# Even tokens first, and a two-phase convolution whose ScalarE/GpSimd taps are all of one sum

## The chip, the core and the metric

The kernel runs on one core of one Trainium2 chip. The metric is the device time of one execution in microseconds (us); lower is better. The core has five engines that run their own instruction queues in order and meet through semaphores: TensorE (PE, with its weight loads shown as PEld), VectorE (DVE), ScalarE (ACT), GpSimd (POOL) and SyncE (SP, which here issues all DMAs). Matrix products land in PSUM, everything else stands in SBUF or in DRAM scratch.

## What is computed

A trunk of two residual layers over 2048 tokens of width 1024, fp32, then a final RMSNorm. Layer 0 is gated linear attention (GLA), layer 1 a causal Conformer convolution module; each has a SiLU gate branch z.

```python
def conv_mixer(h, w_in, dw_w, dw_b, ln_w, ln_b, w_out):
    a, gl, z = jnp.split(h @ w_in, 3, axis=-1)
    u = a * jax.nn.sigmoid(gl)
    u = lax.conv_general_dilated(          # depthwise, causal, 31 taps
        u, dw_w.reshape(CONV_K, 1, CONV_E).astype(u.dtype),
        window_strides=(1,), padding=[(CONV_K - 1, 0)],
        dimension_numbers=('NWC', 'WIO', 'NWC'),
        feature_group_count=CONV_E) + dw_b
    u = jax.nn.silu(layernorm(u, ln_w, ln_b))
    return (u * jax.nn.silu(z)) @ w_out

for i in range(DEPTH):                     # 0: gla_mixer, 1: conv_mixer
    h = rmsnorm(x, norm_w[i])
    y = gla_mixer(h, ...) if i % N_MIXERS == 0 else conv_mixer(h, ...)
    x = x + y
return rmsnorm(x, final_norm_w)
```

The depthwise convolution is done for even and odd tokens apart. With `ue`, `uo` the even and odd tokens of u, A = even taps (16) on `ue`, B = odd taps (15) on `uo`, and C = (even + odd taps, 16) on `ue + uo`: the even outputs are A + B delayed by one, the odd outputs are C - A - B. That is 47 taps over 512 columns in place of 62.

## The kernel before

Activations stand transposed, 128 channels on the partitions and tokens along the free axis, in blocks of 512 tokens (`NB`); the 2048 tokens are two halves (`hf` 0 and 1) of two blocks each (`b`). Every product is done as three fp32r matmuls (hi x hi, hi x lo, lo x hi; `mm3`, line 144), 24 of 128x512 for one 128-channel output block. Weights come in units of 256 columns: a DMA into `wr`, a cast on ACT to `wh` (line 124) and the remainder `wl` on POOL (line 125), two buffers each.

**Layer 0** takes the first 868 us of the trace. In `core`, `turn` transposes each 128-token output `g` on PE into a PSUM bank (line 413), ACT copies it to `st` (line 418) and SP writes it to the scratch `gd` (line 422); head 3 stays in SBUF. `out1` reads it back, projects it, adds x (loaded by line 520) and stores x1 to scratch.

**Layer 1** has, per half, eight `u` units (one channel block of 128 each: `glu`, two projections and a product on DVE, line 754) and four `z` units (`gate_z`, SiLU on ACT, stored to scratch), in the order of `SCHED`. Once a channel block's u is complete (three buffers of u), `conv` puts its convolution on a background list `bg`, in pieces that `pump` hands out against a credit of PE time; LayerNorm goes to a list `bg2` (half 0, run beside half 1's convolution) or `held` (half 1, run beside the output projection). The pieces set only the order in which code is written; a scheduler with its own estimate of times then sets the order of instructions on each engine, with `high_priority` for the projections.

**A channel's convolution** (lines 598 to 677). The first `SIDES[hf][c]` taps of A, and as many of B, are "side" taps: ACT makes the products (line 622), POOL adds them up in `convA`, `convB` (line 624). The rest run on DVE as a chain of scalar_tensor_tensor (line 638) that accumulates in a PSUM bank (`b_bank`, two banks in all), started from the side sum in SBUF (line 642) and ended by writing the sum back to `convA` or `convB`. A comes first, then `ue += uo` (line 669, on POOL in half 0, on DVE in half 1), then B, then the even outputs on POOL (line 647), then C, started by subtracting from `convA` (line 640), and the odd outputs on DVE (line 652). POOL then sums the outputs into `S1` for LayerNorm (line 659).

**The end.** `out2` projects y for half 0, then half 1, adds x1 (`load_x`, line 825, into the buffers u, prod and d), sums squares (lines 842, 844), and `finish` scales by the final RMSNorm (line 864) and stores the block (line 865). LayerNorm of half 1 (lines 700 to 729) and the splitting of its y (line 190) run beside `out2(0, ...)`, on the same DVE, ACT and POOL queues.

## Time and profile before

| | |
|---|---|
| median of 3 runs | 1676.16 us (1675.92 to 1680.72) |
| the profiled execution's own time | 1678.1 us |
| its span in the profile | 1676.0 us |
| PE busy | 1609.4 us (96%) |
| DVE busy | 972.7 us (58%) |
| POOL busy | 900.2 us (54%) |
| ACT busy | 739.6 us (44%) |
| chain that ended last | PE 73%, DVE 16%, DMA 3%, ACT 3% |

Busy shares are means over stages with different limits, so the stretches of layer 1 are read apart further down. A matmul's shown duration overlaps the next one's; the pitch from start to start is what it costs. The same holds for DVE, by less. PEclk is the clock that TensorE was granted, as a share of 2.4 GHz: of its two levels, 1.2 and 2.4 GHz, a mean of 0.96 in a stretch is a mixture.

### The profile page before, as it was taken

Reading aid. Unit: us, or ns where it says so; the run is one execution under the profiler, and the core shown is the slowest. Engines: PE = TensorE matmul, PEld = TensorE weight load, DVE = VectorE, ACT = ScalarE, POOL = GpSimd, SP = SyncE. Lnnn points to the kernel's source line nnn. Section 1 sums busy time; section 2 is a strip of 40 time slices with the busy share of each in tenths; the row PEclk is TensorE's granted clock in tenths of the full one; section 3 lists DMA queues with packets and bytes.
Section 4 is the critical chain, followed back from the end, with each engine's and each line's share of the span. In section 5 each row is a group of like instructions: output and inputs, shape, how many; then the busy total and the mean of one; then the engine's idle time right before and its main releaser. Section 6 shows DMA issues by size and latency. Waiting matters only on the chain.

```text
span 1676.0 us, 23547 instructions
## 1 busy us (share of the span) xinstructions
PE 1609.4 (96%) x9028; PEld 1410.2 (84%) x9028; DVE 972.7 (58%) x1481; ACT 739.6 (44%) x1246; POOL 900.2 (54%) x787
## 2 busy tenths in 40 slices
PE   8999999999999999999999999999999899999697
PEld 6989999998889999999888887877788678877597
DVE  7433232241434232325243999989699999977634
ACT  6645252342557353415232544443553355435432
POOL 4444343334744333323342989985398798456342
PEclk9999999999999999999999999999999999999798
DMA  6021111144511212123452211225154113643633
GB/s 190 26 83 57 64 51 57 57 139 139 169 45 33 82 51 64 45 63 102 144 164 88 76 38 38 94 70 157 59 174 157 57 45 101 202 163 124 234 115 137
DMA packets 74016, 165.68 MB, mean 99 GB/s; under 512 B 7760, under 2 KB 16464, under 8 KB 73904
## 3 DMA queue, kind: packets, MB, share of 16 engines
q1 hardware_dynamic: 73904, 164.19, 30.5%
q8 instruction: 70, 1.15, 0.3%
q14 instruction: 42, 0.34, 0.1%
HBM read 128.51 MB, written 35.65 MB: 98 GB/s over the span
## 4 chain that ended last, share of the span: by engine, by line
PE 73%; DVE 16%; DMA 3%; ACT 3%; issue 2%; POOL 2%; SPq 0%; POOLq 0%; DVEq 0%; ACTq 0%
PE mm L144 63%; DVE pb L638 10%; PE pb L144 3%; PE pb L388 1%; PE pb L390 1%; DVE pb L642 1%; PE pm L379 1%; DMA wr<-in_wall_dram 1%; PE pm L413 1%; DVE u L754 1%; DVE al L190 1%; PE pm L288 1%; POOL acc L205 1%; DMA u<-x_scratch 1%; DVE pb L640 1%
## 5 line engine op out<-in xcount | busy, mean ns | idle before, releaser
L144 PE MATMUL mm<-ah,wh 128*128 128x512 f32 (+1 forms) x1600 | 595.3, 388 | 44.8 <-DVE u L838 20.4
L144 PE MATMUL mm<-al,wh 128*128 128x512 f32 (+1 forms) x1600 | 592.6, 385 | 0.0
L144 PE MATMUL mm<-ah,wl 128*128 128x512 f32 (+1 forms) x1600 | 590.0, 386 | 0.0
L125 POOL TENSOR_TENSOR wl<-wr,wh 128x1024 fp32r<-128x1024 f32 x140 | 344.0, 2471 | 214.9 <-ACT wh L124 208.9
L144 PEld LDWEIGHTS mm<-ah,wh 128*128 128x128 f32 x1600 | 302.3, 190 | 110.1 <-DVE u L838 20.0
L144 PEld LDWEIGHTS mm<-al,wh 128*128 128x128 f32 x1600 | 302.2, 190 | 57.1 <-issue 0.2
L144 PEld LDWEIGHTS mm<-ah,wl 128*128 128x128 f32 x1600 | 301.4, 190 | 58.0 <-issue 0.2
L144 PE MATMUL mm<-wh,ah 128*128 128x256 f32 x896 | 259.2, 289 | 0.0
L144 PE MATMUL mm<-wh,al 128*128 128x256 f32 x896 | 254.7, 284 | 0.0
L144 PE MATMUL mm<-wl,ah 128*128 128x256 f32 x896 | 254.2, 284 | 0.0
L124 ACT ACTIVATE wh<-wr 128x1024 fp32r<-128x1024 f32 x144 | 145.5, 1051 | 140.9 <-PE mm L144 92.4
L638 DVE SCALAR_TENSOR_TENSOR pb<-u,C,pb 128x512 f32<-128x512 f32 x252 | 184.9, 747 | 0.7
L638 DVE SCALAR_TENSOR_TENSOR pb<-u,dwc,pb 128x512 f32<-128x512 f32 x240 | 179.9, 750 | 1.2
L144 PEld LDWEIGHTS mm<-wl,ah 128*128 128x128 f32 x896 | 171.4, 191 | 0.4
L144 PEld LDWEIGHTS mm<-wh,ah 128*128 128x128 f32 x896 | 171.3, 191 | 0.4
L144 PEld LDWEIGHTS mm<-wh,al 128*128 128x128 f32 x896 | 171.3, 191 | 0.0
L622 ACT ACTIVATE prod<-u,C 128x512 f32<-128x512 f32 x148 | 105.5, 721 | 135.7 <-POOL convA L624 68.4
L624 POOL TENSOR_TENSOR convA<-convA,prod 128x512 f32<-128x512 f32 x74 | 98.3, 1329 | 5.7 <-ACT prod L622 1.6
L624 POOL TENSOR_TENSOR convB<-convB,prod 128x512 f32<-128x512 f32 x74 | 98.0, 1325 | 4.0 <-ACT convB L620 0.7
L397 DVE SCALAR_TENSOR_TENSOR S<-S,dec,pb 128x256 f32<-128x256 f32 x56 | 26.8, 479 | 95.4 <-PE pb L144 95.3
L401 POOL TENSOR_TENSOR ss<-ss,e 128x1 f32<-128x1 f32 x64 | 13.4, 209 | 124.4 <-ACT g L400 124.4
L523 DVE TENSOR_TENSOR Q<-mm,Q 128x512 f32<-128x512 f32 x32 | 22.1, 689 | 93.0 <-PE mm L144 78.3
(195 smaller groups left out, 2174.1 us busy)
## 6 DMA issues: line engine op xcount, KB each, us to landing
wr<-in_wall_dram SPq DMA_DIRECT2D x144, 512.0 KB, 4.1
raw<-in_xT_dram SPq DMA_DIRECT2D x32, 256.0 KB, 3.7
Q<-in_xT_dram SPq DMA_DIRECT2D x32, 256.0 KB, 3.2
x_scratch<-Q SPq DMA_DIRECT2D x32, 256.0 KB, 3.1
sz_scratch<-t SPq DMA_DIRECT2D x32, 256.0 KB, 2.3
b<-sz_scratch SPq DMA_DIRECT2D x32, 256.0 KB, 3.5
g_scratch<-st SPq DMA_DIRECT2D x48, 128.0 KB, 1.9
raw<-g_scratch SPq DMA_DIRECT2D x24, 256.0 KB, 3.5
```

Source lines behind the costliest of these rows:

```text
L124: act.activation(wh[:, ks, :], raw, AF.Copy)
L125: (dve if i < 2 else pool).tensor_tensor(wl[:, ks, :], raw, wh[:, ks, :].bitcast(F32), ALU.subtract)
L144: pe.matmul(ps, s, m, start=(i == 0), stop=(i == 3 * n - 1))
L190: dve.tensor_tensor(lo, src, hi.bitcast(F32), ALU.subtract)
L205: eng.tensor_tensor(acc, acc, sq, ALU.add)
L288: pe.matmul(ps, wgs[:, k, :], m, start=(n == 0), stop=(n == 15))
L379: pe.matmul(s_ps[:, 0:192], ki[:, js], Q[:, j].rearrange("p s c -> p (s c)"), start=True, stop=True)
L397: dve.scalar_tensor_tensor(S[h], S[h], dec[:, j:j + 1], kv, ALU.mult, ALU.add)
L523: dve.tensor_tensor(xr, ps, xr, ALU.add)
L622: act.activation(p, src, AF.Copy, scale=w)
L624: pool.tensor_tensor(acc, acc, p, ALU.add)
L638: dve.scalar_tensor_tensor(dstm, src, w, ps, ALU.mult, ALU.add)
```

## The change

Three things are changed together.

1. **Token order.** From layer 0's output on, each block of 512 tokens stands with its 256 even tokens first and its 256 odd ones behind. `turn` makes this order: the PE transpose writes token columns alternately to the two halves of a 256-column field of the PSUM bank. The stores to `gd` go in runs of 128 columns in place of 256, the residual of `out1` is read from `xP`, a second copy of x in the new order that the host makes, and the host puts the result back in order. In layer 1 the product of `glu` then reads and writes contiguous halves, and so does the product with z; before, `glu` wrote even and odd tokens alternately to two rows of u.
2. **Side taps.** All side taps are of A (`SIDES` doubled, but 18 becomes 15 once in each half), and B has none.
3. **Order and place.** B runs first on DVE, started by a tensor_scalar with the bias; then A, whose sum stays in its PSUM bank; then, with no store to `convA`, the even outputs on DVE from that bank (line 648 of the changed kernel), `ue += uo` always on POOL (line 670), and C goes on in the same bank (lines 643 and 637).

```diff
-SIDES = ((1, 7, 7, 7, 7, 5, 9, 7),
-         (1, 5, 3, 5, 9, 7, 6, 4))
+SIDES = ((2, 14, 14, 14, 14, 10, 15, 14),
+         (2, 10, 6, 10, 15, 14, 12, 8))
...
-                o = c * 256 + (i % 2) * P
-                pe.transpose(gt[:, o:o + P], g[:, c * P:(c + 1) * P], ident)
+                o = (i % 2) * CK
+                gv = gt[:, c * 256:(c + 1) * 256].rearrange("p (s t) -> p s t", s=2)[:, :, o:o + CK]
+                pe.transpose(gv.rearrange("p s t -> p t s"), g[:, c * P:(c + 1) * P], ident)
...
-                            out=gd[hf, r0:r0 + P, (i - 1) * P:(i + 1) * P],
-                            in_=st[:, c * 256:(c + 1) * 256])
+                            out=gd[hf, r0:r0 + P, b * NB:(b + 1) * NB].rearrange(
+                                "p (s t) -> p s t", s=2)[:, :, o:o + P],
+                            in_=st[:, c * 256:(c + 1) * 256].rearrange("p (s t) -> p s t", s=2))
...
-                    sp.dma_start(out=xr, in_=xT[ch * P:(ch + 1) * P, t0:t0 + NB])
+                    sp.dma_start(out=xr, in_=xP[ch * P:(ch + 1) * P, t0:t0 + NB])
...
-        def side(which):
-
-            st[which] = l2p.tile([P, NB + 1], F32, name="conv" + which, bufs=2)
-            acc = st["p" + which] = st[which][:, 1:NB + 1]
+        def side():
+
+            acc = st["pA"] = l2p.tile([P, NB], F32, name="convA", bufs=2)
             for m in range(nside):
-                src, w = tap(which, m)
+                src, w = tap("A", m)
                 p = acc if m == 0 else l2p.tile([P, NB], F32, name="prod", bufs=2)
-                if m == 0 and which == "B":
-                    act.activation(p, src, AF.Identity, scale=w, bias=cc(C_DWB, c))
-                else:
-                    act.activation(p, src, AF.Copy, scale=w)
+                act.activation(p, src, AF.Copy, scale=w)
...
-                first = 0 if which == "C" else nside
-                if m0 == first:
-                    st["ps"] = b_bank()
-                ps = st["ps"]
+                first = nside if which == "A" else 0
+                if m0 == first and which != "C":
+                    st["ps" + which] = b_bank()
+                ps = st["ps" + ("B" if which == "B" else "A")]
...
-                    if m == n - 1 and which != "C":
-                        dstm = st["p" + which]
+                    dstm = st["B"][:, 1:NB + 1] if which == "B" and m == n - 1 else ps
...
-                    elif which == "C":
-                        dve.scalar_tensor_tensor(dstm, src, w, st["pA"], ALU.mult, ALU.subtract)
+                    elif which == "A":
+                        dve.scalar_tensor_tensor(dstm, src, w, st["pA"], ALU.mult, ALU.add)
+                    elif which == "B":
+                        dve.tensor_scalar(dstm, src, w, cc(C_DWB, c), ALU.mult, ALU.add)
                     else:
-                        dve.scalar_tensor_tensor(dstm, src, w, st["p" + which], ALU.mult, ALU.add)
+                        dve.scalar_tensor_tensor(dstm, src, w, ps, ALU.mult, ALU.subtract)
...
-            pool.tensor_tensor(d[:, 0], st["pA"], st["B"][:, 0:NB], ALU.add)
+            dve.tensor_tensor(d[:, 0], st["psA"], st["B"][:, 0:NB], ALU.add)
...
-        for which, n in (("A", 16), ("B", 15), ("C", 16)):
-            m0 = 0 if which == "C" else nside
+        for which, n in (("B", 15), ("A", 16), ("C", 16)):
+            m0 = nside if which == "A" else 0
...
-                items.append((0.0, lambda: (pool if hf == 0 else dve).tensor_tensor(ue, ue, uo, ALU.add)))
-            if which == "B":
-                items.append((0.0, even))
+                items.append((0.0, lambda: pool.tensor_tensor(ue, ue, uo, ALU.add)))
+                items.append((0.6, even))
...
-                zv = z.rearrange("p (t s) -> p s t", s=2)
+                zv = wide(z)
...
-                    u[:, :, o:o + 256].rearrange("p s t -> p t s"),
-                    a_ps.rearrange("p (t s) -> p t s", s=2),
-                    sg.rearrange("p (t s) -> p t s", s=2), ALU.mult)
+                    u[:, :, o:o + 256],
+                    a_ps.rearrange("p (s t) -> p s t", s=2),
+                    sg.rearrange("p (s t) -> p s t", s=2), ALU.mult)
```

The order of instructions in layer 0 is the same before and after; only shapes differ there. In layer 1 it moves, and three places matter. In the rows a line number is the kernel's own, so the same statement can have another number before and after (638 and 637, 652 and 653, 669 and 670, 190 and 192, 167 and 169).

DVE in half 0, where one channel's last sum C ends and the next one's begins; before: line 652 is the odd output of a channel, 754 the product of `glu`, 640 the first tap of C, 642 the first tap of A behind the side sum.

```order
L652 SCALAR_TENSOR_TENSOR d<-pb,dwb_96,convB 128x512
L754 TENSOR_TENSOR u<-mm,t_9744 128x256x2
L754 TENSOR_TENSOR u<-mm,t_9820 128x256x2
L638 SCALAR_TENSOR_TENSOR pb<-u,C,pb 128x512
L640 SCALAR_TENSOR_TENSOR pb<-u,dwc,convA 128x512
L638 SCALAR_TENSOR_TENSOR convB<-u,C,pb 128x512
L638 SCALAR_TENSOR_TENSOR pb<-u,dwc,pb 128x512
L642 SCALAR_TENSOR_TENSOR pb<-u,C,convA 128x512
L638 SCALAR_TENSOR_TENSOR pb<-u,dwc,pb 128x512
L638 SCALAR_TENSOR_TENSOR pb<-u,C,pb 128x512
```

The same place of the changed kernel: line 639 is the first tap of A, 648 the even output, 653 the odd output, 641 the first tap of B, 643 the first tap of C.

```order
L639 SCALAR_TENSOR_TENSOR pb<-u,C,convA 128x512
L637 SCALAR_TENSOR_TENSOR pb<-u,dwc,pb 128x512
L637 SCALAR_TENSOR_TENSOR pb<-u,C,pb 128x512
L637 SCALAR_TENSOR_TENSOR pb<-u,dwc,pb 128x512
L648 TENSOR_TENSOR d<-pb,convB 128x512
L637 SCALAR_TENSOR_TENSOR pb<-u,dwc,pb 128x512 x4
L653 SCALAR_TENSOR_TENSOR d<-pb,dwb_96,convB 128x512
L754 TENSOR_TENSOR u<-mm,t_9949 128x2x256
L754 TENSOR_TENSOR u<-mm,t_10024 128x2x256
L641 TENSOR_SCALAR pb<-u,C 128x512
L643 SCALAR_TENSOR_TENSOR pb<-u,dwc,pb 128x512
```

What moved: before, C of a channel began behind B of the same channel, one row into the alternation with the next channel's A; now A, the even output, the rest of the channel before, two products of `glu` and the first tap of the next B stand between A's last tap and C's first, which needs `ue += uo` from POOL.

POOL in half 0, around `ue += uo`; before: line 669 is that addition, 624 the side sums, 647 the even output, 649 a carried column, 125 the weight remainder.

```order
L796 COPY halo<-u 128x30
L669 TENSOR_TENSOR u<-u 128x527
L624 TENSOR_TENSOR convA<-convA,prod 128x512
L647 TENSOR_TENSOR d<-convA,convB 128x512
L649 COPY bcar<-convB 128x1
L624 TENSOR_TENSOR convA<-convA,prod 128x512 x2
L624 TENSOR_TENSOR convB<-convB,prod 128x512 x4
L125 TENSOR_TENSOR wl<-wr,wh 128x1024 x2
```

The same place of the changed kernel: 670 is the addition, 625 the side sums, 650 the carried column, 785 the copy of the halo into a new u, 660 the sum for LayerNorm.

```order
L625 TENSOR_TENSOR convA<-convA,prod 128x512
L650 COPY bcar<-convB 128x1
L625 TENSOR_TENSOR convA<-convA,prod 128x512
L785 COPY u<-halo 128x2x15
L625 TENSOR_TENSOR convA<-convA,prod 128x512
L670 TENSOR_TENSOR u<-u 128x527
L660 TENSOR_TENSOR S_9658<-S_9658,d 128x1024
L676 COPY convB<-bcar 128x1
```

What moved: the even output has left POOL's queue, and the addition stands behind a halo copy and a side tap, where before it had the whole of B's chain between it and the first tap that needs it.

DVE near the end, where `out2` of half 0 finishes its first block (line 167 makes its variance just ahead of the first row here) and LayerNorm of half 1 goes on; before: 727 scales by LayerNorm's factor, 729 multiplies by z, 190 splits y, 844 sums squares, 864 scales and so frees the output block.

```order
L727 TENSOR_TENSOR d<-d,pm 128x2x256 x8
L729 TENSOR_TENSOR b_13753<-b_13753,d 128x2x256
L729 TENSOR_TENSOR b_13812<-b_13812,d 128x2x256
L190 TENSOR_TENSOR al<-b_13753,ah 128x512
L190 TENSOR_TENSOR al<-b_13803,ah 128x512
L190 TENSOR_TENSOR al<-b_13812,ah 128x512
L190 TENSOR_TENSOR al<-b_13821,ah 128x512
L844 TENSOR_TENSOR acc<-acc,pb 128x512 x2
L729 TENSOR_TENSOR b_13830<-b_13830,d 128x2x256
L844 TENSOR_TENSOR acc<-acc,pb 128x512
L729 TENSOR_TENSOR b_13848<-b_13848,d 128x2x256
L864 SCALAR_TENSOR_TENSOR u<-u,C,pb 128x512 x2
```

The same place of the changed kernel: 169 makes the variance, 192 is the split of y, 709 a sum of LayerNorm, 838 adds x1 to a projection.

```order
L169 TENSOR_SCALAR v_14041<-pb 128x4
L192 TENSOR_TENSOR al<-b_13653,ah 128x512
L192 TENSOR_TENSOR al<-b_13666,ah 128x512
L709 TENSOR_TENSOR S_12023<-S_12023,pb 128x2x256
L729 TENSOR_TENSOR b_13721<-b_13721,d 128x512
L192 TENSOR_TENSOR al<-b_13708,ah 128x512
L192 TENSOR_TENSOR al<-b_13721,ah 128x512
L844 TENSOR_TENSOR acc<-acc,pb 128x512 x2
L838 TENSOR_TENSOR d<-mm,d 128x512 x2
L192 TENSOR_TENSOR al<-b_13734,ah 128x512
L864 SCALAR_TENSOR_TENSOR u<-u,C,pb 128x512 x6
```

What moved: the block's scaling (864) came behind LayerNorm's second block (727 x8 and what follows it), and now stands ahead of all of that.

## Rows read from the trace of the kernel before

**Rows 1.** The whole span, by stretch of the program: layer 0 with its projection (0 to 868), half 0 of the convolution (925 to 1225), half 1 (1225 to 1475) and the end with LayerNorm beside the output projection (1475 to 1600). Columns: length, then busy us (and instructions) of each engine, mean granted TensorE clock, DMA share, GB/s. The last row is one slice of 25 us of the same view in which PE was never late.

```profile
0.00:868.00 868.00, 854.94 (x5535) 783.62 (x5535) 310.11 (x562) 385.03 (x737) 353.24 (x407) 1.00 0.28 86
...
925.00:1225.00 300.00, 288.68 (x1248) 236.14 (x1247) 277.22 (x369) 142.76 (x204) 239.81 (x179) 0.98 0.25 80
1225.00:1475.00 250.00, 240.49 (x1052) 197.04 (x1051) 249.97 (x340) 115.94 (x160) 192.15 (x135) 0.99 0.39 127
1475.00:1600.00 125.00, 103.27 (x451) 84.02 (x450) 80.37 (x117) 56.45 (x82) 64.20 (x35) 0.90 0.46 154
...
1050.00:1075.00 25.00, 25.00 (x112) 20.71 (x111) 24.61 (x35) 11.09 (x16) 24.26 (x19) 1.00 0.31 104
```

**Rows 2.** The same view of parts of the convolution: the units of half 0 up to 1100.

```profile
925.00:1100.00 175.00, 172.38 (x759) 141.87 (x758) 172.34 (x234) 86.49 (x122) 164.44 (x127) 1.00 0.20 66
```

**Rows 3.** PE's waits, engine, line and tile waited for, us in total, times, longest; the first row from 925 to 1225, the next from 1225 to 1475, the last from 1475 to 1600.

```profile
PE mm L144 <- DVE u L754: 5.8, 3, 3.2
...
PE mm L144 <- DVE u L754: 6.8, 3, 4.4
...
PE mm L144 <- DVE u L838: 18.2, 3, 16.2
```

**Rows 4.** DVE from 925 to 1475, grouped by line: operation, out<-in, shapes, count, then busy us, mean ns of one, and idle time before them with what ended it.

```profile
L638 DVE SCALAR_TENSOR_TENSOR pb<-u,C,pb 128x512 f32<-128x512 f32 x252 | 184.9, 747 | 0.7
...
L642 DVE SCALAR_TENSOR_TENSOR pb<-u,C,convB 128x512 f32<-128x512 f32 x16 | 26.5, 1654 | 5.2 <-POOL convB L624 5.2
L640 DVE SCALAR_TENSOR_TENSOR pb<-u,dwc,convA 128x512 f32<-128x512 f32 x16 | 26.0, 1626 | 0.0
L642 DVE SCALAR_TENSOR_TENSOR pb<-u,C,convA 128x512 f32<-128x512 f32 x16 | 21.3, 1331 | 0.9 <-ACT convA L622 0.9
...
L669 DVE TENSOR_TENSOR u<-u 128x527 f32<-128x527 f32 x8 | 11.2, 1399 | 0.0
```

**Rows 5.** The same view over the whole span, shapes kept apart: the product of `glu`, a contiguous product of a PSUM and an SBUF operand (line 523), a tensor_scalar of 512 columns with two per-partition scalars (line 313), a sum of an SBUF and a PSUM operand (line 709), and the PE transposes of `turn`.

```profile
L754 DVE TENSOR_TENSOR u<-mm,t 128x512 f32<-128x512 f32 x32 | 33.2, 1071 | 22.8 <-PE mm L144 22.8
L523 DVE TENSOR_TENSOR Q<-mm,Q 128x512 f32<-128x512 f32 x32 | 22.1, 689 | 93.0 <-PE mm L144 78.3 <-DMA Q<-in_xT_dram 14.7
L313 DVE TENSOR_SCALAR Ei<-pm,C 128x512 f32<-128x512 f32 x14 | 9.9, 746 | 2.7 <-ACT tmp L312 2.4
L709 DVE TENSOR_TENSOR S<-S,pb 128x512 f32<-128x512 f32 x16 | 10.8, 685 | 6.8 <-ACT pb L706 4.0 <-POOL S L709 2.7
L413 PE MATMUL pm<-ident,g 128*128 128x128 f32 x128 | 24.4, 272 | 0.0
```

**Rows 6.** The timeline of DVE at the end of half 1's convolution (start, length, engine, line, operation, count): taps of two chains in turn, and then seven of one chain.

```profile
1469.12 0.74 DVE L638 SCALAR_TENSOR_TENSOR pb<-u,C,pb 128x512 f32<-128x512 f32 x1
1469.78 0.74 DVE L638 SCALAR_TENSOR_TENSOR pb<-u,dwc,pb 128x512 f32<-128x512 f32 x1
...
1473.73 5.49 DVE L638 SCALAR_TENSOR_TENSOR pb<-u,dwc,pb 128x512 f32<-128x512 f32 x7
```

**Rows 7.** POOL from 925 to 1475, grouped by line as in rows 4.

```profile
L125 POOL TENSOR_TENSOR wl<-wr,wh 128x1024 fp32r<-128x1024 f32 x50 | 124.4, 2500 | 50.6 <-ACT wh L124 50.6
L624 POOL TENSOR_TENSOR convA<-convA,prod 128x512 f32<-128x512 f32 x74 | 98.3, 1329 | 5.7 <-ACT prod L622 1.6 <-ACT convA L622 0.7
L647 POOL TENSOR_TENSOR d<-convA,convB 128x512 f32<-128x512 f32 x16 | 22.3, 1397 | 27.0 <-DVE convB L638 25.9 <-ACT prod L622 1.2
...
L669 POOL TENSOR_TENSOR u<-u 128x527 f32<-128x527 f32 x8 | 11.1, 1391 | 0.3 <-DVE convA L638 0.3
```

**Rows 8.** POOL's waits ahead of its halo copies from 925 to 1475, columns as in rows 3.

```profile
POOL u L785 <- DVE pb L638: 19.6, 5, 13.9
```

**Rows 9.** PE's timeline in layer 0, around one pair of transposes.

```profile
201.38 0.38 PE L413 MATMUL pm<-ident,g 128*128 128x128 f32 x2
201.51 0.48 PE L144 MATMUL mm<-ah,wl 128*128 128x512 f32 x1
201.82 0.40 PE L144 MATMUL mm<-ah,wh 128*128 128x512 f32 x1
```

**Rows 10.** DVE's timeline near the end, from the first block's variance to the first sum with x1 of the last half.

```profile
1547.89 0.15 DVE L167 TENSOR_SCALAR v<-pb 128x4 f32<-128x4 f32 x1
1548.70 4.87 DVE L727 TENSOR_TENSOR d<-d,pm 128x512 f32<-128x512 f32 x8 [0.66 <-PE pm L178]
...
1570.08 1.39 DVE L864 SCALAR_TENSOR_TENSOR u<-u,C,pb 128x512 f32<-128x512 f32 x2
...
1581.36 1.29 DVE L838 TENSOR_TENSOR u<-mm,u 128x512 f32<-128x512 f32 x2 [1.49 <-DMA u<-x_scratch]
```

**Rows 11.** The chain of waits over the same stretch (start, length, what).

```profile
1570.08 1.41 DVE u L864 x2
...
1571.50 3.56 DMA out_dram<-u
...
1575.08 6.19 DMA u<-x_scratch
...
1581.36 0.70 DVE u L838
```

22 lines of the change are left out of this document (13 added, 9 removed).

## The prediction

> **What bounds the kernel now.** I read the mean busy shares first: PE is at 96% of the span, so no edit of another engine can give back more than PE's late moments and its slow ones. Then the stretches [rows 1]. In layer 0 PE is busy for 854.94 of 868 us while DVE is below half: PE sets the pace, and the change moves no instruction there. In the convolution both are full: from 925 to 1225 PE is busy 288.68 of 300 us and DVE 277.22, and from 1225 to 1475 DVE is busy 249.97 of 250 us. DVE sets the pace there, through the product of `glu` that PE waits for [rows 3]. From 1475 to 1600 PE loses most: it is busy 103.27 of 125 us, and one wait of 16.2 us for `out2`'s sum with x1 is most of it [rows 3].
>
> How much is there to win? A slice where PE was never late holds 112 matmuls in 25 us, 0.2232 us each [rows 1]. At that pitch 925 to 1225 has room for 1344 instructions and holds 1248: 96 x 0.2232 = 21 us lost, of which 11.3 us are idle and the rest is mainly matmuls at the lower clock (granted 0.98). In the same way 1225 to 1475 lost 68 x 0.2232 = 15 us (9.5 us idle) and 1475 to 1600 lost 109 x 0.2232 = 24 us (21.7 us idle, granted 0.90). A few records can be missing and some of those counted are narrower, so the idle times are the lower ends. Together 43 to 60 us are the ceiling.
>
> **DVE, part by part.** In the convolution a tap is shown with 0.747 us [rows 4], but taps of two chains in turn start 0.66 us apart, and seven of one chain take 5.49 us, 0.78 each [rows 6]: a tap that reads what the one ahead wrote pays 0.12 us more.
> - First tap of B: 1.654 us with the side sum in SBUF [rows 4] becomes a tensor_scalar. The nearest row, of the same width with two scalars but from PSUM, is 0.746 us [rows 5]. From SBUF the trace shows none; the ends are 0.4 us (half of that row and a little) and 1.331 us, the cheapest first tap with only SBUF inputs [rows 4]. I take 0.746: 8 x 0.908 = 7.3 us per half.
> - First tap of A keeps its form. First tap of C reads PSUM in place of `convA`: 1.626 us becomes 0.747 [rows 4], 8 x 0.879 = 7.0 us per half.
> - `glu`: 1.071 us with alternating writes, 0.689 for a contiguous product of the same operands [rows 5]: 16 x 0.382 = 6.1 us per half.
> - Added: eight even outputs per half (0.685 us shown [rows 5], about 0.6 in the queue), 4.8 us; side taps fall from 100 to 97 in half 0 and from 80 to 77 in half 1, three more DVE taps each, 2.0 us. By the written order 69 taps stand directly behind the one they read, 57 before: 6 x 0.12 = 0.7 us per half.
> - In half 1 `ue += uo` leaves DVE: 8 x 1.399 = 11.2 us [rows 4].
>
> Half 0: 7.3 + 7.0 + 6.1 - 4.8 - 2.0 - 0.7 = 12.9 us less. Half 1: 12.9 + 11.2 = 24.1 us less.
>
> **POOL and ACT.** A chain's first side product needs no addition, so one chain in place of two saves one in each channel less: 84 additions in half 0 become 97 - 8 = 89, 64 in half 1 become 69. Five more cost 5 x 1.33 = 6.6 us per half; the even outputs leave, 8 x 1.397 = 11.2 us; `ue += uo` comes in half 1, 8 x 1.391 = 11.1 us [rows 7]. Half 0 is 4.6 us lighter, half 1 6.5 us heavier. That weight is covered in half 1, where POOL is busy 192.15 of 250 us [rows 1], and would be paid in full if it came to stand ahead of C. ACT makes six products fewer and has slack: nothing.
>
> **What of it reaches the end.** In half 0 up to 1100, POOL is busy 164.44 of 175 us, nearly as full as DVE with 172.34 [rows 2]. A pace that DVE alone would allow, 12.9 us faster, is held back by POOL, so I take 8 us. In half 1 DVE gives more than PE has to lose; I take 10 us, near the idle 9.5, since some slow-clock time stays.
>
> The new order adds a wait: C's first tap (643) needs `ue += uo` (670), which POOL can do only behind A's last tap. On DVE a tap, the even output, four taps, the odd output, two products and B's first tap stand between: 0.66 + 0.6 + 4 x 0.78 + 0.66 + 1.2 + 0.66, some 7 us. On POOL stand two side additions, a halo copy and the addition itself, 4 us. But the halo copy waits for the u buffer that the channel before frees with its last C tap (such waits cost 19.6 us before [rows 8]); from there POOL needs 1.33 + 1.39 = 2.7 us and DVE has 2.6 us of other work. So it is nearly even, and I charge 0.25 us a channel, 16 x 0.25 = 4 us. The ends are nothing, and two weight remainders of 2.5 us each [rows 7] ahead of it. What queues behind that tap on DVE is the next `glu`, and so PE.
>
> The end: before, the scaling that frees `out2`'s buffers starts 22.2 us behind its variance (1547.89 to 1570.08) because LayerNorm's second block stands ahead of it [rows 10]; store, load and sum then take until 1581.36 [rows 11], and PE has waited 16.2 us [rows 3]. Now eleven instructions of 0.6 to 0.9 us stand between, about 8 us, 14 us less, and LayerNorm's second block comes behind. Of the 16.2 us I take 13; the ends are nothing, if LayerNorm's waits on ACT and on z's load now stand ahead of the last half's sums, and the whole 24 us.
>
> **Layer 0.** 128 transposes write PSUM alternately 1 KB apart. A pair and one matmul take 201.82 - 201.38 = 0.44 us, of which the matmul is 0.23: 0.105 us for one [rows 9], 13.4 us for all, on PE's path. No row shows a scattered write. The ends are nothing and as much again, 13.4 us; per column a transpose already takes twice what a plain matmul does, which leaves the write half of its time, and I take nothing. The Trainium skill, "SBUF — State Buffer", section "Door 1: The DMA port swizzle", says that PSUM is accessed in 8-byte lines and that any non-contiguous PSUM pattern significantly slows matmuls. No row here bears it out or denies it; by that rule the sum would be the second rival's.
>
> The stores of `g` in shorter runs and the loads of `xP` are hidden behind PE: none of its waits in layer 0 that I rest on is a store's, and the transfers move the same bytes.
>
> Sum: 8 + 10 + 13 - 4 = 27 us. The profiled execution took 1678.1 us for a span of 1676.0: 1678.1 - 27 = 1651 us. The median of the runs shown is 1676.16, 2 us lower, which is inside what I can tell.
>
> **Rivals.**
> - POOL holds the convolution: DVE's relief turns into waits for side sums in both halves, and only the end gains. For it: rows 2. Against it: before, DVE waited for a side sum hardly at all (5.2 and 0.9 us [rows 4]), and now B's whole chain covers the sum of A. 1678 - 13 = 1665 us.
> - The scattered transposes cost as much again: 1651 + 13.4 = 1664 us.
> - No change: the end's wait only moves to LayerNorm's waits, and the convolution gains no more than the new waits cost. 1678 us; against it speaks that DVE is full for 250 us.
> - Slower: C's first tap waits for `ue += uo` behind two weight remainders in every channel, 2 x 2.5 = 5 us x 16 = 80 us, less 37 us of relief and 13 us at the end: 1678 + 30 = 1708 us. It decides from (37 + 13) / 16 = 3.1 us a channel. For it: `ue += uo` in half 1 was on DVE and waited for nobody; against it: the written order puts no remainder between halo copy and addition in most channels of half 0.
>
> **How the numbers follow.** Forecast 1651 us, 0.55; POOL holds 0.14; transposes 0.10; no change 0.09; slower 0.12. About 0.3%, 5 us, is what a measurement of this kernel can tell from no change. Faster is 0.55 + 0.14 + 0.10 = 0.79, less 0.01 for the third's edge: 0.78; same 0.09 + 0.01 = 0.10; slower 0.12. The range begins where both halves and the end gain nearly all of their ceilings less the new waits, 1678 - 13 - 15 - 20 + 4 = 1634, and goes to 1676, which leaves out the slower rival and half of no change.
>
> **What would show it.** Right: the first C tap near 0.75 us, `glu` near 0.69, the first B tap below 0.8; PE idle from 925 to 1475 below 10 us in place of 20.8; no wait for x1 over 5 us at the end; transposes at 272 ns with unchanged pitch. Wrong: DVE waiting for POOL at C's first tap more than 2 us a channel, layer 0 later than 868 us by ten or more, or PE waiting behind LayerNorm's second block in the last half.

## The result and the profile after

The changed kernel takes 1647.14 us (median of four runs, 1645.75 to 1651.64) beside 1676.04 us for the kernel before in the same comparison. The ratio is 0.983, with a 95% interval of 0.980 to 0.986: 29 us less. Forecast were 1651 us, in a range of 1634 to 1676. The profiled execution has a span of 1649.5 us against 1676.0, so 26.5 us are to be found in the traces.

The stretches of [rows 1] in the changed kernel (length, busy us and instructions of PE, PEld, DVE, ACT, POOL, granted clock, DMA share, GB/s):

```profile
0.00:868.00 868.00, 855.36 (x5545) 783.98 (x5546) 310.48 (x563) 384.63 (x737) 354.43 (x407) 1.00 0.28 86
...
925.00:1225.00 300.00, 292.25 (x1290) 240.06 (x1289) 278.01 (x403) 152.41 (x214) 238.53 (x184) 0.99 0.28 88
1225.00:1475.00 250.00, 243.47 (x1060) 199.42 (x1059) 231.17 (x330) 110.41 (x151) 189.88 (x136) 0.99 0.37 123
1475.00:1600.00 125.00, 118.17 (x581) 100.58 (x580) 89.41 (x130) 61.56 (x92) 68.53 (x36) 0.95 0.54 183
```

Layer 0 is unchanged. In half 1 DVE is no longer full: 231 of 250 us where it was 250. In the last of these stretches PE is idle 6.8 us where it was 21.7. What PE waits for shows the same. Columns as in [rows 3]; the first two rows are from 925 to 1225, the next from 1225 to 1475, the last three from 1475 on:

```profile
PE mm L146 <- ACT t L767: 3.4, 2, 2.7
PE mm L146 <- ACT t L750: 2.5, 2, 1.8
...
PE mm L146 <- DVE u L838: 4.1, 1, 4.1
...
PE mm L146 <- DVE d L838: 4.5, 2, 4.1
PE pb L168 <- DVE acc L844: 3.7, 2, 2.6
...
PE mm L146 <- DVE u L838: 1.6, 1, 1.6
```

No wait for the product of `glu` (754) is left, and the 16.2 us for x1's sum (838) are 1.6. DVE in the convolution, as in [rows 4]:

```profile
L639 DVE SCALAR_TENSOR_TENSOR pb<-u,C,convA 128x512 f32<-128x512 f32 x16 | 19.8, 1238 | 0.5 <-POOL convA L625 0.5
L754 DVE TENSOR_TENSOR u<-mm,t 128x512 f32<-128x512 f32 x29 | 19.4, 684 | 5.2 <-PE mm L146 4.0 <-ACT t L750 1.0
...
L641 DVE TENSOR_SCALAR pb<-u,C 128x512 f32<-128x512 f32 x15 | 12.1, 805 | 0.1
L643 DVE SCALAR_TENSOR_TENSOR pb<-u,dwc,pb 128x512 f32<-128x512 f32 x16 | 12.0, 751 | 8.2 <-POOL u L670 8.2
```

B's first tap takes 0.805 us (1.654 before), C's first 0.751 (1.626), the product of `glu` 0.684 (1.071). The new wait is there: C's first tap waits 8.2 us in all for `ue += uo` on POOL.

Three places in DVE's timeline cut the 26.5 us into pieces: the first product of half 1, the last odd output of the convolution (653), and the final scaling that frees the output block (864).

```profile
1198.29 1.29 DVE L754 TENSOR_TENSOR u<-mm,t 128x512 f32<-128x512 f32 x2 [0.18 <-PE mm L146]
...
1467.45 0.75 DVE L653 SCALAR_TENSOR_TENSOR d<-pb,dwb,convB 128x512 f32<-128x512 f32 x1
...
1518.68 0.15 DVE L169 TENSOR_SCALAR v<-pb 128x4 f32<-128x4 f32 x1
...
1527.33 4.09 DVE L192 TENSOR_TENSOR al<-b,ah 128x512 fp32r<-128x512 f32 x2 [3.97 <-ACT ah L191]
...
1534.48 0.68 DVE L192 TENSOR_TENSOR al<-b,ah 128x512 fp32r<-128x512 f32 x1
1535.08 4.03 DVE L864 SCALAR_TENSOR_TENSOR u<-u,C,pb 128x512 f32<-128x512 f32 x6
...
1548.14 4.87 DVE L727 TENSOR_TENSOR d<-d,pm 128x512 f32<-128x512 f32 x8 [3.57 <-PE pm L180]
```

The first two of these places in the kernel before (the third is in [rows 10]):

```profile
1204.80 2.07 DVE L754 TENSOR_TENSOR u<-mm,t 128x512 f32<-128x512 f32 x2 [1.07 <-PE mm L144]
...
1481.31 0.75 DVE L652 SCALAR_TENSOR_TENSOR d<-pb,dwb,convB 128x512 f32<-128x512 f32 x1
```

Half 1 begins 6.5 us earlier, the convolution ends at 1468.2 in place of 1482.1, 13.9 us earlier, and from there to the end it is 181.3 us in place of 193.9, 12.6 us less. The scaling comes at 1535.08 against 1570.08 [rows 10] and ahead of LayerNorm's second block (1548.14), behind which it stood before.

### The profile page after: what moved, and what is told of

Read it like the earlier page. It is cut to its first block, busy times and chain, and to the rows that moved or that the text cites. A ratio compares the mean times of both kernels' runs of the same rounds, so it can differ in the third digit from the quotient of the medians.

```text
span 1649.5 us, 23586 instructions
## 1 busy us (share of the span) xinstructions
PE 1603.0 (97%) x9028; PEld 1407.4 (85%) x9028; DVE 950.6 (58%) x1495; ACT 739.7 (45%) x1244; POOL 888.7 (54%) x789
## 4 chain that ended last, share of the span: by engine, by line
PE 80%; DVE 5%; DMA 5%; ACT 4%; issue 3%; POOL 2%; SPq 0%; POOLq 0%; DVEq 0%; ACTq 0%
PE mm L146 70%; PE pb L146 3%; DMA wr<-in_wall_dram 2%; DVE al L192 2%; PE pb L390 1%; PE pb L392 1%; PE pm L381 1%; DVE pb L637 1%; DMA raw<-x_scratch 1%; POOL wl L127 1%; PE pm L416 1%; PE pm L290 1%; DVE d L727 1%; DMA t<-x_scratch 1%; POOL acc L207 1%
## 5 line engine op out<-in xcount | busy, mean ns | idle before, releaser
L625 POOL TENSOR_TENSOR convA<-convA,prod 128x512 f32<-128x512 f32 x158 | 207.0, 1312 | 11.6 <-ACT prod L623 4.9
L637 DVE SCALAR_TENSOR_TENSOR pb<-u,C,pb 128x512 f32<-128x512 f32 x274 | 199.5, 747 | 1.0
L623 ACT ACTIVATE prod<-u,C 128x512 f32<-128x512 f32 x158 | 112.7, 721 | 105.0 <-POOL convA L625 104.6
L443 DVE SCALAR_TENSOR_TENSOR vl<-mm,r,vh 128x256 fp32r<-128x256 f32 x48 | 22.9, 483 | 89.3 <-ACT vh L442 89.2
```

What stands on the lines that cost most here:

```text
L443: dve.scalar_tensor_tensor(vl, ps, rr, vh.bitcast(F32), ALU.mult, ALU.subtract)
L623: act.activation(p, src, AF.Copy, scale=w)
L625: pool.tensor_tensor(acc, acc, p, ALU.add)
L637: dve.scalar_tensor_tensor(dstm, src, w, ps, ALU.mult, ALU.add)
```

## The experiments

The theory at the outset: DVE's shorter work lets PE wait less in the convolution, and the new place of the scaling removes the long wait at the end. The main rivals: one of the two parts of the change alone does it; DVE's time is hidden and only the order of the instructions counts. For each kernel two numbers are read beside its time: where the convolution ends (start of its last odd output plus its length) and how long the rest of the span is. Both are of the one profiled execution, which can lie off the median: 4.6 us above it in run 4, 4.5 above in the changed kernel, 4.9 below in run 7, within about 2 us in the others. The kernel before was measured again beside each group of runs and took 1675.4 to 1676.8 us, so differences of about 2 us between runs tell nothing.

| kernel | median us | end of convolution | rest of the span | scaling against LayerNorm's second block |
|---|---|---|---|---|
| before | 1676.0 | 1482.1 | 193.9 | behind |
| 1 token order alone | 1670.3 | 1476.5 | 193.2 | behind |
| 5 `ue += uo` on DVE | 1665.5 | 1470.9 | 191.7 | behind |
| 7 A's sum in SBUF | 1672.6 | 1467.2 | 198.7 | behind |
| 4 before, scaling first | 1665.7 | 1484.0 | 184.4 | ahead |
| 9 changed, scaling earlier still | 1656.3 | 1468.1 | 186.0 | ahead |
| 10 as 7, scaling first | 1654.3 | 1471.9 | 180.7 | ahead |
| 11 B's first tap from SBUF | 1657.2 | 1477.1 | 177.1 | ahead |
| 12 odd output twice | 1656.7 | 1479.1 | 174.1 | ahead |
| 3 odd output four times | 1680.0 | 1507.2 | 168.7 | ahead |
| 8 third product buffer | 1648.6 | 1471.1 | 177.7 | ahead |
| 6 as 5, scaling first | 1647.6 | 1468.3 | 178.7 | ahead |
| 2 convolution alone | 1648.2 | 1467.5 | 178.7 | ahead |
| changed | 1647.1 | 1468.2 | 181.3 | ahead |

**1. The token order alone.** The kernel before with every hunk of the change outside `conv` and `SIDES`, as in

```diff
-                o = c * 256 + (i % 2) * P
-                pe.transpose(gt[:, o:o + P], g[:, c * P:(c + 1) * P], ident)
+                o = (i % 2) * CK
+                gv = gt[:, c * 256:(c + 1) * 256].rearrange("p (s t) -> p s t", s=2)[:, :, o:o + CK]
+                pe.transpose(gv.rearrange("p s t -> p t s"), g[:, c * P:(c + 1) * P], ident)
...
-                    u[:, :, o:o + 256].rearrange("p s t -> p t s"),
+                    u[:, :, o:o + 256],
```

> The kernel before with the token order alone (even tokens first from layer 0's output on, so the gated product, the sums of layer 1 and the normalisation read and write whole rows; the transposes write their columns alternately); the convolution, its side taps and its chains stay as they were, and on VectorE the scaling of the last half's first block still stands behind the second normalisation block, as before. My theory (VectorE's shorter work lets TensorE wait less in the convolution, and a changed place of the scaling takes away the 16.2 us wait at the end): only the gated product gets cheaper (1.071 to 0.685 us, 32 times, 12 us of VectorE), so a third of the gain in the convolution, some 4 to 6 us, and the 16.2 us wait on L838 stays at 10 us or more: 1668 to 1674 us. Rival, the token order is the whole change: 1647 to 1652 us. Rival, the alternate columns cost TensorE time that the convolution's gain hides: above 1676 us, with transposes whose pitch is over 0.105 us.

1670.32 us, ratio 0.997 (0.996 to 0.998). The convolution ends 5.6 us earlier, and the wait at the end stays. PE's waits from 1475 on:

```profile
PE mm L145 <- DVE u L842: 15.7, 1, 15.7
```

The first theory's number. The token order is not the whole change, and its scattered transposes cost nothing that could be seen.

**2. The convolution alone.** The kernel before with the hunks in `conv` and `SIDES`:

```diff
-                        dve.scalar_tensor_tensor(dstm, src, w, st["pA"], ALU.mult, ALU.subtract)
+                        dve.scalar_tensor_tensor(dstm, src, w, ps, ALU.mult, ALU.subtract)
...
+                        dve.tensor_scalar(dstm, src, w, cc(C_DWB, c), ALU.mult, ALU.add)
...
-        for which, n in (("A", 16), ("B", 15), ("C", 16)):
+        for which, n in (("B", 15), ("A", 16), ("C", 16)):
```

> The kernel before with the convolution's part alone: side taps of A only, B's chain first, A's sum kept in PSUM; the token order stays (tokens interleaved). On VectorE the scaling of the last half's first block now stands ahead of the second normalisation block, as in the changed kernel. My theory: the convolution's gain less the gated product's part, some 9 to 13 us over both halves, and the end's 9 to 13 us whole: 1650 to 1658 us, with no wait on L838 above 6 us. Rival, the token order gives most: above 1665 us. Rival, the convolution's VectorE time is hidden and only the place of the scaling counts: 1662 to 1668 us.

1648.22 us, ratio 0.984 (0.982 to 0.987): all of the gain, more than I expected. The token order makes the `glu` product cheaper by 0.39 us 32 times, 12 us, and on top of the new convolution this is worth 1 us, which cannot be told from nothing. The convolution ends no later for these 12 us (1467.5 and 1468.2).

**3. 34 us more for DVE.** The changed kernel with

```diff
-            dve.scalar_tensor_tensor(
-                dst[c][:, 1], st["psA"], dwb2[:, c:c + 1], st["B"][:, 1:NB + 1], ALU.add, ALU.subtract)
+            for _ in range(4):
+                dve.scalar_tensor_tensor(
+                    dst[c][:, 1], st["psA"], dwb2[:, c:c + 1], st["B"][:, 1:NB + 1], ALU.add, ALU.subtract)
```

> The changed kernel with each channel's last VectorE operation of the convolution (the odd tokens' combination) issued four times instead of once, with the same operands: 48 more VectorE operations of about 0.7 us, 34 us, 17 in each half's convolution, which is about what the change took from VectorE there. The place of the scaling at the end stays as in the changed kernel. My theory: the convolution's gain (17 us against before) goes nearly whole, the end's stays: 1658 to 1668 us, with TensorE's idle time in 925 to 1475 us up by 10 us or more. Rival, VectorE's work in the convolution lies beside TensorE's and the gain is from the order of instructions or the end alone: 1645 to 1651 us. Rival, VectorE sets the pace of the convolution outright: 1647 + 34 = 1681 us.

1680.00 us, the number of the last rival: the 34 us cost 33. In its timeline the convolution ends at 1507.2, 39 us later than in the changed kernel, and although the scaling stands ahead of LayerNorm's second block it comes so late that PE waits 16.4 us for x1's sum again. DVE's timeline, and PE's wait from 1475 on:

```profile
1504.04 3.12 DVE L654 SCALAR_TENSOR_TENSOR d<-pb,dwb,convB 128x512 f32<-128x512 f32 x4
...
1573.18 2.05 DVE L865 SCALAR_TENSOR_TENSOR u<-u,C,pb 128x512 f32<-128x512 f32 x3
...
1584.74 4.86 DVE L728 TENSOR_TENSOR d<-d,pm 128x512 f32<-128x512 f32 x8
```

```profile
PE mm L146 <- DVE u L839: 19.5, 3, 16.4
```

So the wait at the end is a matter of how late DVE is as well as of what stands where, and the rival that DVE's time is hidden is out. In the convolution PE is idle 26.5 us where it was 14.3, as my theory had said. It does not wait for the product of `glu` there (1.8 us in all) but for ACT's gates (768) and sigmoids (751), from 925 to 1475:

```profile
PE mm L146 <- ACT t L768: 12.5, 7, 5.9
PE mm L146 <- ACT t L751: 8.2, 5, 3.9
```

In the same stretch POOL's halo copy into a new u waits 21.8 us for DVE's taps (13.1 in the changed kernel), and ACT's first side products wait 14.0 us for that copy. That DVE's delay comes to PE by this way is read from these waits; no run tried it.

**4. The kernel before, with the scaling first.** Only the priority of the final normalisation of the first written block is raised:

```diff
-                with tc.high_priority(offset=1000 if ns > 1 else 0):
+                with tc.high_priority(offset=1000 if ns > 1 or hf == b == 0 else 0):
...
+                with tc.high_priority(offset=1000 if hf == b == 0 else 0):
                 for ch, m, t in parts:
```

> The kernel before, in which only the final normalisation of the first block of tokens written (its variance and its scaling) is given a higher priority, so that on VectorE the eight scalings stand ahead of the second normalisation block of layer 1, as in the changed kernel; everything else stays. My theory: the 16.2 us wait on L838 falls below 6 us, 8 to 14 us of it reach the end: 1662 to 1668 us. Rival, the wait is TensorE's spare time, which is waited elsewhere (on the second normalisation's splits): 1674 to 1677 us, with the wait moved to L754, L767 or the output projection's next tiles. Rival, the whole gain of the change is this order: 1647 to 1652 us.

1665.73 us, ratio 0.995 (0.994 to 0.996): 10 us, with the convolution as late as before. PE's waits from 1475 on:

```profile
PE pb L166 <- DVE acc L844: 12.2, 3, 10.4
PE pb L178 <- POOL r4f L168: 4.1, 2, 3.1
PE mm L144 <- DVE u L838: 2.0, 2, 1.1
```

The long wait is gone from x1's sum, but a new one of 10.4 us stands at the sum of squares (844). On DVE it now queues behind the block that was moved back:

```profile
1553.98 4.02 DVE L865 SCALAR_TENSOR_TENSOR u<-u,C,pb 128x512 f32<-128x512 f32 x6
...
1561.44 3.07 DVE L727 TENSOR_TENSOR d<-d,pm 128x512 f32<-128x512 f32 x5
...
1566.83 4.31 DVE L729 TENSOR_TENSOR b<-b,d 128x512 f32<-128x512 f32 x2
1571.06 0.67 DVE L844 TENSOR_TENSOR acc<-acc,pb 128x512 f32<-128x512 f32 x1
```

The place of the scaling is worth 10 us on the old convolution, net of that.

**5 and 6. `ue += uo` on DVE in half 1, and the same with the scaling first.** The changed kernel with

```diff
-                items.append((0.0, lambda: pool.tensor_tensor(ue, ue, uo, ALU.add)))
+                items.append((0.0, lambda: (pool if hf == 0 else dve).tensor_tensor(ue, ue, uo, ALU.add)))
```

> The changed kernel with the addition of odd to even tokens (ue += uo) back on VectorE in the second half, as before: 8 operations of 1.40 us, 11 us more for VectorE, 11 less for GpSimd, and the wait of C's first tap for GpSimd there (5.4 us) gone. In this version the scaling of the first written block stands behind the second normalisation block again. My theory (VectorE has about 12 us of room in the convolution of the changed kernel, since the gated product's 12 us cost nothing with the old token order, and the place of the scaling is worth 10 us): the convolution ends within 3 us of the changed kernel's, a wait of 8 us or more on L838 comes back, 1654 to 1660 us. Rival, each us of VectorE in the convolution costs a us: 1664 to 1670 us. Rival, the place of the scaling matters only together with a late convolution: 1646 to 1651 us.

> As the run with ue += uo on VectorE in the second half, and the variance and scaling of the first written block with a higher priority, so that they stand ahead of the second normalisation block. My theory: the wait on L838 goes again, 1646 to 1651 us, 8 us or more below its twin. Rival, each us of VectorE costs a us: 1656 to 1660 us. Rival, the place of the scaling is worth nothing here: the same as its twin.

The second has the priority of run 4 as well. 1665.45 and 1647.62 us. Their convolutions end 2.6 us apart; the place of the scaling is worth 17.8 us. Where they go in run 5 shows in PE's timeline, and in the stretch around it:

```profile
1557.50 2.08 PE L180 MATMUL pb<-ident,r4f 128*128 128x128 f32 x8 [10.40 <-POOL r4f L170]
...
1570.32 0.80 PE L146 MATMUL mm<-ah,wh 128*128 128x512 f32 x1 [10.73 <-DVE u L838]
```

```profile
1550.00:1575.00 25.00, 6.76 (x22) 5.56 (x23) 20.12 (x31) 4.97 (x9) 7.22 (x4) 0.53 1.01 369
```

PE loses 10 us twice: to a broadcast of the second written block's factor, which needs a variance that stands on DVE behind LayerNorm's second block and the eight scalings, and then to x1's sum. DVE's timeline in run 5:

```profile
1540.43 4.87 DVE L727 TENSOR_TENSOR d<-d,pm 128x512 f32<-128x512 f32 x8 [2.41 <-PE pm L180]
...
1554.03 0.14 DVE L169 TENSOR_SCALAR v<-pb 128x4 f32<-128x4 f32 x1
```

In run 6 the first is 4.4 us in three pieces, and the sum in the freed buffers (`u`) is no longer waited for. Run 6's convolution ends where the changed kernel's does (1468.3 and 1468.2): neither the 11 us that `ue += uo` costs DVE in half 1 nor the 5.4 us of C's wait that it takes away (2.8 of 8.2 are left) leaves a mark there.

**7 and 10. A's sum in SBUF again.** The changed kernel with

```diff
-                    dstm = st["B"][:, 1:NB + 1] if which == "B" and m == n - 1 else ps
+                    dstm = ps
+                    if m == n - 1 and which != "C":
+                        dstm = st["B"][:, 1:NB + 1] if which == "B" else st["pA"]
...
-                        dve.scalar_tensor_tensor(dstm, src, w, ps, ALU.mult, ALU.subtract)
+                        dve.scalar_tensor_tensor(dstm, src, w, st["pA"], ALU.mult, ALU.subtract)
...
-            dve.tensor_tensor(d[:, 0], st["psA"], st["B"][:, 0:NB], ALU.add)
+            pool.tensor_tensor(d[:, 0], st["pA"], st["B"][:, 0:NB], ALU.add)
```

and run 10 with the priority of run 4 besides.

> The changed kernel with one piece undone: A's last tap writes its sum to SBUF, C's first tap reads it there, and the even tokens' sum is GpSimd's again. VectorE: 16 first taps at about 1.6 instead of 0.75 us (14 us more), 16 sums of 0.68 less (11 us), 3 us more; GpSimd 16 x 1.33 = 21 us more. The scaling stands behind the second normalisation block in this version. My theory: VectorE's 3 us lie in its room and only the place of the scaling costs: 1655 to 1662 us. Rival, GpSimd holds the convolution (its side taps come late, VectorE waits at L639 or at L643): 1664 us or more, with over 10 us of VectorE waiting for GpSimd. Rival, this piece is the whole gain of the convolution: 1670 us or more.

> The run with A's sum in SBUF again, with the higher priority for the variance and scaling of the first written block. In its twin the convolution ended as early as in the changed kernel. My theory: the whole loss of its twin came from the place of the scaling, 1646 to 1652 us. Rival, the 21 us that GpSimd has more to do hold back the normalisation and the weight remainders: 1656 us or more.

1672.63 and 1654.26 us. The first is in the last rival's range, but the trace says something else: its convolution ends 1 us earlier than the changed kernel's, although C's first tap takes 1.845 us and waits 10 us for POOL.

```profile
L645 DVE SCALAR_TENSOR_TENSOR pb<-u,dwc,convA 128x512 f32<-128x512 f32 x16 | 29.5, 1845 | 10.3 <-POOL u L672 10.2
```

All of the loss lies behind the convolution, and the place of the scaling takes 18 of it back. Run 10 was expected at 1646 to 1652 and is 2 us above; against run 9, which has the same priority, it is 2 us below. Keeping A's sum in PSUM is not what made the convolution faster: its return moved the end by 1 us forward (run 7) and by 3.8 us back (run 10 against run 9).

**8. A third buffer for the side products**, and so for the load of x1 that shares it (`load_x`).

```diff
-                p = acc if m == 0 else l2p.tile([P, NB], F32, name="prod", bufs=2)
+                p = acc if m == 0 else l2p.tile([P, NB], F32, name="prod", bufs=3)
...
-                    t = l2p.tile([P, 1, NB], F32, name="prod", bufs=2)
+                    t = l2p.tile([P, 1, NB], F32, name="prod", bufs=3)
```

> The changed kernel with a third buffer for the products of the side taps. In the changed kernel ScalarE waits 104.6 us at L623 in 925 to 1475 us for GpSimd to free one, in front of sigmoids and gates for which TensorE waits 8.1 us (L750, L767). My theory: part of these 8.1 us goes, 1640 to 1645 us. Rival, GpSimd sets the pace of the side taps and a third buffer only moves ScalarE's wait: 1646 to 1649 us. Rival, ScalarE's run ahead pushes GpSimd's weight remainders back: above 1650 us, with TensorE waiting on L127.

1648.63 us: the second theory's number. ACT's wait for POOL falls from 104.6 to 90.6 us, and PE's waits for ACT (750, 767) from 8.1 to 6.2, without a gain in time. An attempt to beat the changed kernel that did not.

**9. The changed kernel with the scaling earlier still.** The edit is that of run 4, on the changed kernel.

> The changed kernel with the higher priority for the variance and scaling of the first written block; the scaling, which already stood ahead of the second normalisation block, comes some rows earlier. My theory (TensorE's remaining waits at the end are for the second normalisation's products and the last sums, 1.6 us for the scaled tile alone): 1644 to 1648 us, no difference that can be measured. Rival, the 16.4 us between its variance and the scaling still hold TensorE back: 1636 to 1643 us. It is also the base for the other runs of this group.

1656.34 us, 9 us slower than the changed kernel: no theory had that. The scaling begins at 1524.48, 10.6 us earlier than in the changed kernel; the convolution ends at the same time. DVE's timeline:

```profile
1524.48 4.03 DVE L865 SCALAR_TENSOR_TENSOR u<-u,C,pb 128x512 f32<-128x512 f32 x6
...
1541.10 0.69 DVE L838 TENSOR_TENSOR u<-mm,u 128x512 f32<-128x512 f32 x1 [1.07 <-DMA wr<-in_wall_dram]
...
1551.99 0.68 DVE L838 TENSOR_TENSOR u<-mm,u 128x512 f32<-128x512 f32 x1
...
1562.47 2.01 DVE L729 TENSOR_TENSOR b<-b,d 128x512 f32<-128x512 f32 x1 [5.78 <-DMA b<-sz_scratch]
...
1569.17 1.28 DVE L838 TENSOR_TENSOR u<-mm,u 128x512 f32<-128x512 f32 x2
```

The first of x1's sums is earlier (1541.10; 1552.93 in the changed kernel), but the third and fourth now stand behind LayerNorm's products (729) and splits, and so behind a load of z: 1569.17, where the changed kernel had four done by 1561.6. PE's wait for this sum is 3.2 us. The time from the convolution's end to the end of the span is 186.0 us, in place of 181.3. That this place is what costs the 9 us was not tried, and the profiles account for 4.6 of them, since the changed kernel's was the slowest of its four executions.

Run 6 has the same priority and differs from run 9 only by `ue += uo` on DVE in half 1. It takes 1647.62 us, 8.7 less, although DVE has 11 us more to do; the convolutions end at the same time (1468.3 and 1468.1), and the rest of the span is 178.7 us against 186.0. In it the third and fourth sum come at 1562.11:

```profile
1562.11 1.29 DVE L838 TENSOR_TENSOR u<-mm,u 128x512 f32<-128x512 f32 x2 [0.94 <-PE mm L146]
```

So the higher priority need not cost anything. What run 9 loses against run 6 lies behind the convolution, where the two have the same instructions in another order.

**11 and 12. B's first tap with a bias tile from SBUF, and the odd output twice.** Both have run 9's priority, and run 9 was meant as their base. Run 11:

```diff
-                        dve.tensor_scalar(dstm, src, w, cc(C_DWB, c), ALU.mult, ALU.add)
+                        dve.scalar_tensor_tensor(dstm, src, w, st["B"][:, 1:NB + 1], ALU.mult, ALU.add)
...
+        act.activation(st["B"][:, 1:NB + 1], uo[:, 1:1 + NB], AF.Identity, scale=0.0, bias=cc(C_DWB, c))
```

and run 12 is run 3 with `range(2)`.

> The changed kernel with the higher priority as above, in which B's first tap adds a bias tile in SBUF again (written by ScalarE for each channel) in place of the bias column: 16 operations of about 1.65 in place of 0.81 us, 13 us more for VectorE, and 16 small activations for ScalarE. Theory that B's cheap first tap carries the convolution's gain: the convolution ends 6 us or more later, 1654 to 1661 us. Theory that VectorE has 12 us of room there: the convolution ends within 3 us, 1646 to 1651 us.

> The changed kernel with the higher priority as above and each channel's odd sum issued twice, with the same operands: 16 more VectorE operations of 0.74 us, 12 us. Theory of 12 us of room: 1646 to 1651 us. Theory that VectorE sets the pace outright (34 us in 48 operations cost 33 us): 1656 to 1660 us.

1657.22 and 1656.71 us. Taken by their ranges they name the theory without room, but those ranges were set for a base of 1647. Against run 9 with its 1656.34 they cost 0.9 and 0.4 us; against run 6, which has the same priority, and against the changed kernel they cost 9 to 10. Which base is the right one these runs do not say, since run 9's end is in an order of its own. What they do show is that the convolution ends later than in run 9, by 9 and 11 us: 12 us of DVE at these two places are not free there, as the 12 us of `glu` (run 2) and the 11 us of `ue += uo` (run 6) were. The rest of the span is shorter than run 9's by as much. From run 11:

```profile
L641 DVE SCALAR_TENSOR_TENSOR pb<-u,C,convB 128x512 f32<-128x512 f32 x16 | 24.7, 1545 | 11.4 <-ACT convB L677 11.4
```

The tap itself costs 12.6 us more and waits 11.4 us for ACT's tile, which the changed kernel doesn't have; how much of the 9 us is the one and how much the other stays open.

## Why the prediction was right, point by point

- **The durations.** C's first tap (0.747 taken, 0.751 measured), `glu` (0.689, 0.684) and POOL's additions (158 forecast, 158 counted in 925 to 1475) came out. B's first tap was taken from a row that read PSUM, 0.746, and takes 0.805 from SBUF: 1 us over 16.
- **Half 0: 8 less 2 for the waits; half 1: 10 less 2.** By the landmarks 6.5 us at half 1's first product and 13.9 at the convolution's end, so 7.4 in half 1: the sizes that the sum had. That DVE's time there counts is shown by run 3. Runs 2, 5 to 7 and 10 correct the parts: A's sum in PSUM (14 us of DVE by my count, less 10 for the even output that comes with it), the 12 us of `glu` and the 11 us of `ue += uo` can each be given back, alone, for at most 4 us of the convolution's end (run 10; the third buffer of run 8 moved it by 2.9). B's cheap first tap is the one piece whose return moved that end much, by 9 us, with run 11's reservation. B's chain first and the side taps all of A no run took out, so which piece made the convolution faster stays open. The pieces don't add, and a us of DVE has no one price: 12 us of `glu` (run 2) moved the end by less than 1 us, 12 us at the odd output (run 12) by 11.
- **What the convolution is worth in time, 14 us net of the waits.** I took an earlier convolution as so much less in time. With the scaling behind, it is so in run 5 (11.2 us earlier than before, 11 us less) and run 1 (5.6 and 5), and not in run 7 (14.9 and 4). With the scaling ahead, run 4 has the old convolution, and runs 9 and 6 have the new one with the same priority: 9.4 us less in run 9, 18.1 in run 6, with the same end of the convolution. So the runs put this term between 4 and 18 us, by the order that the end happens to get; 14 is neither borne out nor refuted.
- **The new waits, 4 us.** 8.2 us on DVE, twice the forecast. They stay on DVE: no wait of PE for `glu` is left in the changed kernel, and in run 6, which has 2.8 us of them, the convolution ends no earlier.
- **The end, 13 us.** By the landmark 12.6 us. Of the working only the mechanism stands. I had the scaling about 8 us behind its variance; it comes 16.4 us behind (1518.68 to 1535.08), since the splits between them wait 3.97 us for ACT and two of them take 4.09. It saves 5.8 us there, not 14. That the wait still went comes from the variance itself, which is 29.2 us earlier (1547.89 [rows 10] to 1518.68): DVE reaches it earlier, and it no longer stands as late in the order. Runs 4, and 6 against 5, show the place of the scaling alone to be worth 10 and 18 us, and run 9 shows that another order of the same end gives 9 us back. How the 29 us divide depends on the way one goes. By runs 4 and 9 the place of the scaling is worth 10 us, the convolution 9, and the last 9 are fortune of the order; by runs 4 and 6 the first two are 10 and 18, with nothing left over; by runs 5 and 6 the convolution comes first with 11 and the place has 18. The sum of 27 us came out. How much of it is the convolution's (9 to 18 on these ways, 14 in the sum) and how much the end's (10 to 19, 13 in the sum) stays open. That the end's 13 came near the landmark is in part luck, since its own working (8 us from variance to scaling, 14 saved) did not hold.
- **Layer 0, 0 us.** Right. The prediction says that the transposes write 1 KB apart; it is 512 B, 128 columns of 4 bytes. By [rows 9] a pair and its matmul took 201.82 - 201.38 = 0.44 us; in the changed kernel it is 201.70 - 201.25 = 0.45, and each transposition takes the same 272 ns.

```profile
201.25 0.38 PE L416 MATMUL pm<-ident,g 128*128 128x128 f32 x2
201.38 0.48 PE L146 MATMUL mm<-ah,wl 128*128 128x512 f32 x1
201.70 0.40 PE L146 MATMUL mm<-ah,wh 128*128 128x512 f32 x1
```

  The rule of the Trainium skill, "SBUF — State Buffer", section "Door 1: The DMA port swizzle", that any non-contiguous PSUM pattern significantly slows matmuls, is not borne out for these writes.
- **The signs to look for.** PE's idle time from 925 to 1475 is 14.3 us, not below 10 as I had said: of the waits, 8.1 us for ACT's sigmoids and gates stay, which I had left out, and 4.1 for x1's sum. The scaling's place and B's first tap missed by the sizes above; the other signs came as told.
- **The rivals.** POOL does not hold the convolution: with 21 us more on it the end moves by 1 us forward (run 7) or 3.8 us back (run 10). The slower one needed 3.1 us a channel at C's first tap; it is 0.5.

## What to carry to other kernels

Where two engines are nearly balanced, do not add up the relief of the fuller one as if each us had the same price: with the new convolution, 12 us of DVE's `glu` were worth 1 us, and about as many at another place of the same queue moved the convolution's end by 11. Look at what stands behind what on an in-order engine near the end: one eight-instruction block ahead of or behind another was worth 10 to 18 us, as much as all arithmetic saved, and it can be tested by itself with a priority. A scheduler gives such an order away as a side effect of any edit: runs 6 and 9 differ in one addition a channel of half 1, their convolutions end together, and their times differ by 9 us. So compare the orders first, put no edit's name on a gain before a run has held the order fixed, and try a test on more than one base.

## What the runs showed of the hardware

The same VectorE operation with two SBUF operands took very different times. In the changed kernel's timeline above, two splits of y (192) take 4.09 us from 1527.33 on, and the next alone 0.68 us at 1534.48. GpSimd in the same stretch:

```profile
1526.81 1.29 POOL L729 TENSOR_TENSOR b<-b,d 128x512 f32<-128x512 f32 x1
...
1528.05 2.82 POOL L127 TENSOR_TENSOR wl<-wr,wh 128x1024 fp32r<-128x1024 f32 x1
...
1535.06 2.38 POOL L127 TENSOR_TENSOR wl<-wr,wh 128x1024 fp32r<-128x1024 f32 x1 [4.18 <-ACT wh L126]
```

GpSimd is busy until 1530.87 beside the slow pair and idle beside nearly all of the fast one; its weight remainder takes 2.82 us beside the pair and 2.38 at 1535.06. The scalings from 1535.08 on, which read one operand in PSUM, keep their 0.67 us beside the same weight remainder. The Trainium skill, "SBUF — State Buffer", section "SBUF: two separate sides", says that VectorE operations with two SBUF inputs and GpSimd's that read SBUF take turns at a shared port pair, whole instructions at a time; these rows agree. The first taps show the same. Of A's first taps in the changed kernel (639, side sum in SBUF, mean 1.24 us) the three that met no GpSimd instruction took 0.75 us each, the other thirteen 1.35 on average. The kernel before shows it at C's first tap (640): 0.75 for the three alone, 1.83 on average for the thirteen beside GpSimd. The changed kernel's C tap (643), with one operand in PSUM, took 0.74 to 0.76 in either case. So what the change saved on C's first taps is time beside a busy GpSimd.

TensorE's clock at work, in run 5: in the slice 1550 to 1575, which holds the end of the first wait of 10 us and all of the second, the granted clock is 0.53. The first matmuls behind the second wait start 0.42 us apart, which is the pace of 1.2 GHz, and from 1573.76 on 0.23 us, that of 2.4 GHz:

```profile
1570.91 0.63 PE L146 MATMUL mm<-al,wh 128*128 128x512 f32 x1
1571.33 0.63 PE L146 MATMUL mm<-ah,wl 128*128 128x512 f32 x1
...
1573.76 0.39 PE L146 MATMUL mm<-ah,wl 128*128 128x512 f32 x1
1573.99 0.40 PE L146 MATMUL mm<-ah,wh 128*128 128x512 f32 x1
```

From the first matmul behind the wait (1570.32) to 1573.76 eight of them take 3.44 us, where eight at 0.23 would take 1.84: this wait of 10.7 us cost 1.6 us more behind itself.
